# Latent keys through DRAM, and another order of the gate and up products

## The chip, the cores and the metric

The kernel runs on one core of a Trainium2 chip. The core has a matrix engine (TensorE, "PE" in the profile, with its weight loads shown apart as "PEld"), a vector engine (VectorE, DVE), a scalar engine (ScalarE, ACT), a general engine (GpSimd, POOL), and SyncE (SP), which issues all of this kernel's DMA transfers. The engines run beside each other and wait for each other through semaphores; each works through its own instructions in order. The metric is the device time of one execution in microseconds (us).

## The reference

Two layers work on `x` (1024 positions x 1024 columns, float32). Each has a mixer with three head groups (sliding-window attention A, latent attention B, spatial gating C) and a feed-forward block. The change touches group B and the first half of the feed-forward block:

```python
def mla(c_q, c_kv, k_rope, q_norm_w, w_uq, kv_norm_w, w_ukv, cos, sin):
    q = (rms_norm(c_q, q_norm_w) @ w_uq).reshape(b_, s_, 6, 64 + 32)
    q_nope, q_rope = q[..., :64], apply_rope(q[..., 64:], cos, sin)
    kv = (rms_norm(c_kv, kv_norm_w) @ w_ukv).reshape(b_, s_, 6, 64 + 64)
    k_nope, v = kv[..., :64], kv[..., 64:]
    k_r = apply_rope(k_rope[:, :, None, :], cos, sin)[:, :, 0, :]   # one for all heads
    ...
    sc = (q_nope . k_nope + q_rope . k_r) * 96 ** -0.5   # causal, then softmax, then times v

h = rms_norm(x, norm2_w[l]) * (1.0 + sc2) + sh2
gate, up = jnp.split(h @ w_gate_up[l], 2, axis=-1)       # 1024 x (2 x 2816)
x = x + g2 * ((jax.nn.silu(gate) * up) @ w_down[l])
```

`c_q` has 384 columns, `c_kv` 256, `k_rope` 32.

## The kernel before

**Number format.** Each float32 operand of a matmul is split in two parts, h (a rounded copy, by ScalarE) and lo (the rest, by VectorE: the operation in L139), and a product is three matmuls, h*h, h*lo, lo*h (`mm3`, L134 to L136).

**Who sets the order.** The stages are written as generators ("sequences"); hand-written strings of letters (`PRU0`, `PRU1` for the up-projection stage of layer 0 and 1, `PRB0`, `PRB1` for the heads stage) say which one makes its next step, and `need` pulls forward the steps that one depends on. The program is built from these steps by a planner that knows the buffers, so that the order on an engine can differ somewhat from the written one. Buffers come from pools with a fixed number of slots: `G` (33 slots of 4 KB in each partition), `W` (12), `R` (4), `SM` and `AD` (4 each), and eight PSUM banks (`PA`; four and two pairs, `PB`, in the heads stage).

**Up-projection of group B** (letters c, q, l, e, x, y). `ckv_seq` makes `c_kv` and `k_rope` of a tile of 128 positions (288 columns) and the factor `rs_kv` of its norm, and turns `k_rope`. `load_cq` fetches `c_q` from DRAM. `low_rank_t` (L803) transposes a tile's `c_q` (three blocks) and `c_kv` (two) on TensorE and splits them: `lowq`, `lowk`. `up_q` (L816) multiplies by `w_uq` and writes the queries, scaled by `rs_q` and turned, into `QK[t]`, with positions on partitions. `up_kv` (L830) does so with `w_ukv`: half 0 gives the keys of all heads (96 columns each for heads 0 and 1, with the turned `k_rope` copied in by GpSimd, L843; 64 for the others), which go into `QK[t]` beside the queries; half 1 gives the values, which are split into `vB`. Letter x steps through (t, half) of `up_q`, letter y through (t, half) of `up_kv`. `load_up` loads and splits the weights.

**Heads stage** (letters H, S, T, M). There are twelve groups: heads 0 to 5 with the second half of the queries (Q = 1, all 1024 keys), then heads 0 to 5 with the first half (Q = 0, 512 keys). `head_prep` (L1140) makes a group's operands with features on partitions: for each half of the keys that it needs, four transposes out of `QK` into a PSUM bank (`qkTB`, L1159), a rounded copy (L1160) and a subtraction (L139); and the same for the queries. `b_soft` makes the scores (`sB`) and the exponentials, `b_av` their transposes (`pTB`) and the product with `vB`. Keys of Q = 1 lie in two fixed buffers `kT1[h % 2]`, those of Q = 0 in `kT0[h % 2]`; group g is prepared once the scores of group g - 2 are written. The same stage loads x, `ya` and the output weights `wo`.

**Gate and up.** The product is done in 11 pairs of column blocks by a scheme of seven block products in place of eight. `left` (L1406) yields the seven left operands in order, with GpSimd subtracting or adding in place between them; `gu_prep` (L1461) splits each into `gus`; `gu_pair` (L1482) takes the products 0 to 6 with the right operands b11, b21, t3, t2, t1, b22, t4, each for gate and up (12 matmuls each). Products 0, 3, 4, 5 add up in banks `yy`, 1 has banks `xx`, 2 and 6 share `vv`. After 0 the sums are copied to `p1`; after 1 they are added to it and finished (Silu, multiply, store); after 3 copied to `u2` (L1523); after 4 copied to `u4` (L1528), added to `vv` and finished; after 5 finished; after 6 added to `u2` and finished. `want_gu` prepares weights some products ahead (`AHEAD`), and in `pair_steps` the hook `ahead` also runs two background jobs: `bg` (layer 0 only: loads `ada_w` and multiplies it up on VectorE, L256) and `bg2` (`wd_early`, splits down-projection weights into DRAM). The weights of the next pair are loaded in the fourth step of a pair into the four `R` slots (`gur`): `r0` holds a11 and a21, `r1` a12 and a22. Pair 0 runs within the heads strings (letter s).

Of the kernel before, what the change touches and what calls it, by code (L numbers as in the profile page):

```python
# [15 lines left out]
P = 128  # L16
# [50 lines left out]
EY = (1, 0, 1, 1, 0, 0, 0, 1)  # L67
AHEAD = (4, 2, 6, 10, 7, 9, 9)
# [10 lines left out]
def tile_trunk(ctx, tc, x, c, positions, ada_w, ada_b, norm1_w, w_in, a_sinks, b_q_norm_w, b_w_uq,  # L79
# [296 lines left out]
    cqd = [[dr.tile([P, 384], F32, name=f"cq{l}_{t}") for t in range(NT)] for l in range(DEPTH)]  # L376
    yad = [[dr.tile([P, 3, 512], F32, name=f"ya{l}_{hf}") for hf in range(2)] for l in range(DEPTH)]
# [175 lines left out]
    def layer(l, x_tiles):  # L553
# [228 lines left out]
        def load_up(k):  # L782
# [3 lines left out]
            DMA.dma_start(out=raw, in_=src[l, kk * P:(kk + 1) * P, :])  # L786
# [12 lines left out]
        def load_cq(t):  # L799
            cqs[t] = SM([P, 384], F32, "cqr")  # L800
            DMA.dma_start(out=cqs[t], in_=cqd[l][t])

        def low_rank_t(t):  # L803
            cq = cqs.pop(t)
            ck = ckv_tile(t)[:, 0:256]
            hq = G([P, 2, 3, P], F32R, "lowq")
            hk = AD("lowk", [P, 2, 2, P], F32R)
            for src, n, d in ((cq, 3, hq), (ck, 2, hk)):
                pv = PA("lowT").rearrange("p (b f) -> p b f", f=P)
                for k in range(n):  # L810
                    PE.transpose(pv[:, k, :], chunk(src, k), ident)
                ACT.copy(out=d[:, 0], in_=pv[:, :n, :])
                sub(DVE, d[:, 1], pv[:, :n, :], f32(d[:, 0]))
            low[t] = hq, hk

        def up_q(t, hf):  # L816
            d = low[t][0]
            if hf == 0:
                QK.append(G([P, 1024], F32, "QK"))
# [3 lines left out]
            for k in range(3):  # L823
                mm3(ps[:, :288], d[:, 0, k], d[:, 1, k], wuq[k][0][:, cs], wuq[k][1][:, cs], k == 0, k == 2)
# [5 lines left out]
        def up_kv(t, hf):  # L830
            d = low[t][1]
            g = QK[t]
            kd = g[:, 576:768].rearrange("p (h e) -> p h e", h=2)
            r = rs_kv[:, t:t + 1]
            ps = PA("ukv")
            for k in range(2):
                wv = [w.rearrange("p (h e) -> p h e", h=6)[:, :, hf * 64:hf * 64 + 64] for w in wukv[k]]
                mm3(ps[:, :384], d[:, 0, k], d[:, 1, k], wv[0], wv[1], k == 0, k == 1)
            if hf == 0:
# [232 lines left out]
        def cq_seq():  # L1072
            for t in range(NT):
                load_cq(t)
                yield
# [707 lines left out]
```

## Time and profile before

| | us |
|---|---|
| median of 3 runs | 2370.89 (2370.7 to 2372.88) |
| the profiled execution | 2370.5 |
| its span, first to last instruction | 2368.8 |
| TensorE busy | 2258.4 |
| VectorE busy | 1775.4 |
| ScalarE busy | 1120.9 |
| GpSimd busy | 984.8 |
| mean granted TensorE clock | 0.983 of full |

"Busy" of TensorE counts the latency of a matmul, so neighbouring matmuls overlap; the price of one more matmul is the distance from start to start. A row of waits reads: engine, tile and line that waited, what released it, microseconds in all, times, the longest. A row of windows reads: the stretch, then busy microseconds (and instructions) of PE, PEld, DVE, ACT, POOL, the granted clock, the DMA share and GB/s. A row in order of time reads: start, duration, engine, line, operation, how many in a row, and in brackets the idle time before it and its releaser. A row of a tile gives the shortest, median and longest duration in ns, first and last start, and the shapes.

### The profile page before, as it was taken

How to read it: one execution, taken by the hardware profiler on the slowest of the kernel's cores; microseconds unless marked ns; L12 is line 12 of the kernel's file. 1: busy time of each engine (PE TensorE's matmuls, PEld its weight loads, DVE VectorE, ACT ScalarE, POOL GpSimd, SP SyncE). 2: the span in 40 equal slices, each digit the busy share in tenths (PEclk: the TensorE clock that was granted, in tenths of full speed). 3: DMA queues.
4: the chain of work that ended last, by engine and by line, in shares of the span. 5: the costliest groups of instructions: out<-in, count | busy, mean ns of one | idle time of the engine just before them, and what ended most of it. 6: DMA issues, size and time to landing. Idle time of an engine off the chain costs nothing. (4 is left out here: it accounts for less than half of the span.)

```text
span 2368.8 us, 31988 instructions
## 1 busy us (share of the span) xinstructions
PE 2258.4 (95%) x11191; PEld 1904.2 (80%) x11191; DVE 1775.4 (75%) x2793; ACT 1120.9 (47%) x2296; POOL 984.8 (42%) x997
## 2 busy tenths in 40 slices
PE   5999899999999999999999899999999999999998
PEld 4789798887888777878878788988878888887786
DVE  7787578848767777699974875687588767638978
ACT  4566377636344344323344654784564444432233
POOL 4766630322323324545554655212224334225643
PEclk9999999999999999999999999999999999999999
DMA  6503432212566565862240253222134544468433
GB/s 255 167 19 110 175 132 90 90 54 89 173 213 232 186 232 187 319 253 89 80 158 19 62 172 143 81 81 98 54 110 177 180 169 169 171 223 287 150 109 114
DMA packets 155397, 347.66 MB, mean 147 GB/s; under 512 B 12522, under 2 KB 71652, under 8 KB 155236
## 3 DMA queue, kind: packets, MB, share of 16 engines
q1 hardware_dynamic: 155236, 345.62, 42.2%
q8 instruction: 88, 1.44, 0.3%
q14 instruction: 73, 0.60, 0.1%
HBM read 250.65 MB, written 94.92 MB: 146 GB/s over the span
## 5 line engine op out<-in xcount | busy, mean ns | idle before, releaser
L139 DVE TENSOR_TENSOR gus<-gur,gus 128x512 fp32r<-128x512 f32 x264 | 248.3, 961 | 60.3 <-ACT gus L142 59.5
L142 ACT CAST gus<-gur 128x512 fp32r<-128x512 f32 x264 | 160.7, 624 | 209.7 <-PE gate L136 77.0
L134 PE MATMUL gate<-hTh,gus 128*128 128x512 f32 x616 | 243.9, 396 | 15.2 <-ACT hTh L142 8.1
L134 PE MATMUL down<-dnt,dns 128*128 128x512 f32 x616 | 241.8, 393 | 11.5 <-issue 6.0
L134 PE MATMUL up<-hTh,gus 128*128 128x512 f32 x616 | 241.1, 391 | 3.8 <-ACT u L1528 3.8
L135 PE MATMUL down<-dnt,dns 128*128 128x512 f32 x616 | 241.1, 391 | 1.3 <-DVE dnt L139 1.3
L135 PE MATMUL gate<-hTl,gus 128*128 128x512 f32 x616 | 241.7, 392 | 0.1
L136 PE MATMUL gate<-hTh,gus 128*128 128x512 f32 x616 | 241.2, 392 | 0.0
L136 PE MATMUL down<-dnt,dns 128*128 128x512 f32 x616 | 240.7, 391 | 0.0
L136 PE MATMUL up<-hTh,gus 128*128 128x512 f32 x616 | 240.4, 390 | 0.0
L135 PE MATMUL up<-hTl,gus 128*128 128x512 f32 x616 | 240.2, 390 | 0.0
L1435 POOL TENSOR_TENSOR gur<-gur 128x512 f32<-128x512 f32 x44 | 65.2, 1482 | 398.8 <-DVE gus L139 369.5
L142 ACT CAST dns<-act 128x512 fp32r<-128x512 f32 x132 | 81.8, 622 | 248.6 <-PE down L136 189.6
L1613 DVE TENSOR_TENSOR x<-x,down 128x512 f32<-128x512 f32 x224 | 148.0, 679 | 28.9 <-PE down L136 28.6
L134 PEld LDWEIGHTS gate<-hTh,gus 128*128 128x128 f32 x616 | 116.9, 190 | 43.4 <-ACT u L1523 10.0
L139 DVE TENSOR_TENSOR dns<-act,dns 128x512 fp32r<-128x512 f32 x132 | 136.3, 1047 | 15.5 <-ACT dns L142 15.3
L134 PEld LDWEIGHTS down<-dnt,dns 128*128 128x128 f32 x616 | 116.2, 189 | 38.5 <-issue 6.8
L134 PEld LDWEIGHTS up<-hTh,gus 128*128 128x128 f32 x616 | 116.1, 189 | 28.7 <-ACT u L1528 4.9
L135 PEld LDWEIGHTS down<-dnt,dns 128*128 128x128 f32 x616 | 116.5, 189 | 25.8 <-DVE dnt L139 1.7
L135 PEld LDWEIGHTS gate<-hTl,gus 128*128 128x128 f32 x616 | 116.8, 190 | 25.2 <-DVE hTl L139 1.5
L136 PEld LDWEIGHTS gate<-hTh,gus 128*128 128x128 f32 x616 | 116.7, 189 | 24.5
L136 PEld LDWEIGHTS down<-dnt,dns 128*128 128x128 f32 x616 | 116.5, 189 | 24.5
(415 smaller groups left out, 6132.8 us busy)
## 6 DMA issues: line engine op xcount, KB each, us to landing
gur<-in_w_gate_up_dram SPq DMA_DIRECT2D x88, 512.0 KB
ada<-in_ada_w_dram SPq DMA_DIRECT2D x80, 512.0 KB
wp<-wpe SPq DMA_DIRECT2D x77, 512.0 KB
dnt<-wp SPq DMA_DIRECT2D x77, 512.0 KB
dnr<-in_w_down_dram SPq DMA_DIRECT2D x44, 512.0 KB
act<-act SPq DMA_DIRECT2D x44, 512.0 KB
wr<-in_w_in_dram SPq DMA_DIRECT2D x24, 512.0 KB
act<-u SPq DMA_DIRECT2D x44, 256.0 KB
```

What stands on the lines that cost most here:

```text
L134: PE.matmul(ps, lh, rh, start=start, stop=False, skip_group_check=more)
L135: PE.matmul(ps, lh, rl, start=False, stop=False, skip_group_check=more)
L136: PE.matmul(ps, ll, rh, start=False, stop=stop, skip_group_check=more)
L139: eng.tensor_tensor(out=out_, in0=a, in1=b, op=ALU.subtract)
L142: ACT.copy(out=h, in_=src)
L1435: return lambda o, a, b, op: eng.tensor_tensor(out=o, in0=a, in1=b, op=op)
L1613: DVE.tensor_tensor(out=av_, in0=av_, in1=ps[t], op=ALU.add)
```

## The change

**Keys.** `load_cq` scales `c_kv` in place by `rs_kv`. `low_rank_t` transposes also `k_rope` and stores its split to DRAM (`krd`); the split `c_kv` goes into buffers of four tiles (`kls`). `up_kv` is replaced by `up_v` (values of one tile) and `up_k` (128 features, that is two heads, of four tiles: weights stationary, 512 positions moving, so features come out on partitions), which splits the result and stores it to DRAM (`kd`). `head_prep` loads keys from `kd` and, for heads 0 and 1, `krd`; it transposes the queries only. The letter y steps through four values and three key chunks, twice: 14 steps where there were 16. `w_ukv` is loaded with keys and values apart.

**Gate and up.** Products run in the order 0, 2, 3, 1, 4, 6, 5 (pair 0: 0, 1, 2, 3, 4, 6, 5). After 2 the sum is copied to `v2`, to which 4 is added; `u4` is gone. The last product of a pair (5) is issued after the first of the next. `bg` runs in the first four steps of a pair.

```diff
+ORD = ((0, 1, 2, 3, 4, 6, 5), (0, 2, 3, 1, 4, 6, 5))
...
+    kd = [dr.tile([2, 384, S], F32, name=f"kd{l}") for l in range(DEPTH)]
+    krd = [dr.tile([2, 32, S], F32, name=f"krd{l}") for l in range(DEPTH)]
...
+                for a in range(2):
+                    DMA.dma_start(out=raw[:, 384 * a:384 * a + 384].rearrange("p (h e) -> p h e", h=6),
+                                  in_=src[l, kk * P:(kk + 1) * P, :].rearrange("p (h a e) -> p h a e", h=6, a=2)[:, :, a, :])
...
         def load_cq(t):
             cqs[t] = SM([P, 384], F32, "cqr")
             DMA.dma_start(out=cqs[t], in_=cqd[l][t])
+            ck = ckv_tile(t)[:, 0:256]
+            DVE.tensor_scalar(out=ck, in0=ck, scalar1=rs_kv[:, t:t + 1], scalar2=None, op0=ALU.mult)
...
         def low_rank_t(t):
...
+            pv = PA("lowT").rearrange("p (b f) -> p b f", f=P)
+            for k in range(2):
+                PE.transpose(pv[:, k, :], chunk(ck, k), ident)
+            PE.transpose(pv[:32, 2, :], ck[:, 256:288], ident)
+            ACT.copy(out=kh[:, :, ts_], in_=pv[:, :2, :])
+            sub(DVE, kl[:, :, ts_], pv[:, :2, :], f32(kh[:, :, ts_]))
+            ACT.copy(out=hq[:32, 6], in_=pv[:32, 2, :])
+            sub(DVE, hq[:32, 7], pv[:32, 2, :], f32(hq[:32, 6]))
+            DMA.dma_start(out=krd[l][:, :, t * P:(t + 1) * P].rearrange("a p f -> p a f"), in_=f32(hq[:32, 6:8]))
...
+        def up_v(t):
+            kh, kl = kls[t // 4]
+            ts_ = slice(t % 4 * P, (t % 4 + 1) * P)
+            ps = PA("uv")
+            for k in range(2):
+                mm3(ps[:, :384], kh[:, k, ts_], kl[:, k, ts_], wukv[k][0][:, 384:], wukv[k][1][:, 384:], k == 0, k == 1)
+            v = G([P, 6, 2, 64], F32R, "vB")
...
+        def up_k(hf, c):
+
+            kh, kl = kls[hf]
+            ps, cs = PA("uk"), slice(c * P, (c + 1) * P)
+            for k in range(2):
+                mm3(ps, wukv[k][0][:, cs], wukv[k][1][:, cs], kh[:, k, :], kl[:, k, :], k == 0, k == 1)
+            kk = G([P, 2, 512], F32R, "kk")
+            ACT.copy(out=kk[:, 0], in_=ps)
+            sub(DVE, kk[:, 1], ps, f32(kk[:, 0]))
+            DMA.dma_start(out=kd[l][:, cs, hf * 512:(hf + 1) * 512].rearrange("a p f -> p a f"), in_=f32(kk))
...
+        def up_kv_seq():
+            need("e", 5)
+            for hf in range(2):
+                for t in range(4 * hf, 4 * hf + 4):
+                    need("l", t + 1)
+                    up_v(t)
+                    yield
+                for c in range(3):
+                    up_k(hf, c)
                     yield
...
+            for i, dst in enumerate((kh, kl)):
+                if h < 2:
+                    DMA.dma_start(out=f32(dst[64:96]), in_=krd[l][i, :, :512 * (Q + 1)])
+                DMA.dma_start(out=f32(dst[:64]), in_=kd[l][i, 64 * h:64 * h + 64, :512 * (Q + 1)])
+            for _ in range(Q + 1):
+                yield
+            pq = PA("qkTB")
+            for i in range(4):
+                PE.transpose(pq[:96, i * P:(i + 1) * P], QK[Q * 4 + i][:, h * 96:(h + 1) * 96], ident)
+            ACT.copy(out=q2[:96, 0], in_=pq[:96])
+            sub(DVE, q2[:96, 1], pq[:96], f32(q2[:96, 0]))
+            yield
...
+                elif i == 2:
+                    for m in range(2):
+                        v2[m] = SM([P, 512], F32, "v2")
+                        ACT.copy(out=v2[m], in_=vv[m])
+                elif i == 3:
+                    for m in range(2):
+                        u2[m] = SM([P, 512], F32, "u2")
+                        ACT.copy(out=u2[m], in_=yy[m])
+                elif i == 4:
+                    for m in range(2):
+                        DVE.tensor_tensor(out=v2[m], in0=v2[m], in1=yy[m], op=ALU.add)
+                    finish(v2[0], v2[1], 1, 1)
...
-                    if 7 * (j - 1) + i < 9 or i in (1, 3, 4, 6):
+                    if 7 * (j - 1) + i < 9 or i < 4:
...
+        def first_products(g, n):
+
+            for _ in range(2 * n):
+                run(g)
+                yield
+            open_pair.append(g)
...
         for j in range(1, NJ):
-            drain(pair_steps(j))
+            g = pair_steps(j)
+            run(g, 2)
+            drain(open_pair.pop())
+            drain(first_products(g, 5))
+        drain(open_pair.pop())
```

More of the change, by code (lines that the diff above doesn't have):

```diff
@@ new lines, in up_v @@
+        def up_v(t):
+            kh, kl = kls[t // 4]
+            ts_ = slice(t % 4 * P, (t % 4 + 1) * P)
+            ps = PA("uv")
+            for k in range(2):
+                mm3(ps[:, :384], kh[:, k, ts_], kl[:, k, ts_], wukv[k][0][:, 384:], wukv[k][1][:, 384:], k == 0, k == 1)
+            v = G([P, 6, 2, 64], F32R, "vB")
+            vB.append(v)
+            pv = ps[:, :384].rearrange("p (h e) -> p h e", h=6)
+            ACT.copy(out=v[:, :, 0, :], in_=pv)
+            sub(DVE, v[:, :, 1, :], pv, f32(v[:, :, 0, :]))
@@ L1150, in head_prep @@
             heads[h, Q] = (q2[:, 0], q2[:, 1], kh, kl)
-            q0 = h * 96
-            k0 = 576 + 96 * h if h < 2 else 768 + 64 * (h - 2)
-            kn = 96 if h < 2 else 64
-            todo = [(hf, k0, kn, kh[:, hf * 512:hf * 512 + 512], kl[:, hf * 512:hf * 512 + 512])
-                    for hf in range(Q + 1)] + [(Q, q0, 96, q2[:, 0], q2[:, 1])]
-            for hf, c0, n, dh, dl in todo:
-                pq = PA("qkTB")
-                for i in range(4):
-                    PE.transpose(pq[:n, i * P:(i + 1) * P], QK[hf * 4 + i][:, c0:c0 + n], ident)
-                ACT.copy(out=dh[:n], in_=pq[:n])
-                sub(DVE, dl[:n], pq[:n], f32(dh[:n]))
-                yield
+            for i, dst in enumerate((kh, kl)):
[3 more added lines that the diff above has]
+            for _ in range(Q + 1):
+                yield
+            pq = PA("qkTB")
[4 more added lines that the diff above has]
+            yield
         def b_soft(h, n, sm, pr):
@@ L1459, in load_gu, with gu_prep @@
             return r
-        def gu_prep(raws):
+        def gu_prep(raws, order):
             gens = []
@@ L1504, in finish @@
                 DMA.dma_start(out=actd[l][2 * j + m][:, b, :], in_=g)
-            yy = banks()
-            yield from products(0, "b11", yy, True)
-            for m in range(2):
-                ACT.copy(out=p1[:, m, :], in_=yy[m])
-            yield
-            xx = banks()
-            yield from products(1, "b21", xx, True)
-            for m in range(2):
-                DVE.tensor_tensor(out=p1[:, m, :], in0=p1[:, m, :], in1=xx[m], op=ALU.add)
-            finish(p1[:, 0, :], p1[:, 1, :], 0, 0)
@@ L1516, in gu_pair @@
-            yield
-            vv = banks()
-            yield from products(2, "t3", vv, True)
-            yield
-            yield from products(3, "t2", yy, False)
-            for m in range(2):
-                u2[m] = SM([P, 512], F32, "u2")
-                ACT.copy(out=u2[m], in_=yy[m])
-            yield
-            yield from products(4, "t1", yy, False)
-            for m in range(2):
-                u4[m] = SM([P, 512], F32, "u4")
-                ACT.copy(out=u4[m], in_=yy[m])
-            for m in range(2):
-                DVE.tensor_tensor(out=u4[m], in0=u4[m], in1=vv[m], op=ALU.add)
```

143 lines of the change are left out of this document (69 added, 74 removed).

## The prediction

> **What bounds the kernel now.** I read the page first (busy shares), then 10 and 60 us windows to find stages with gaps, then TensorE's waits by stage, then single tiles and the order of time for the price of one instruction.
>
> ```profile
> span 2368.8 us, 31988 instructions
> PE 2258.4 (95%) x11191; PEld 1904.2 (80%) x11191; DVE 1775.4 (75%) x2793; ACT 1120.9 (47%) x2296; POOL 984.8 (42%) x997
> 360.00:420.00 60.00, 59.76 (x395) 51.34 (x394) 51.41 (x111) 47.82 (x101) 4.91 (x5) 1.00 0.26 89
> ```
>
> TensorE works in 95% of the span; 110 us are gaps. In the heads stage of layer 0 (third row, columns span, PE, PEld, DVE, ACT, POOL, clock, DMA) it has no gaps, so there an instruction taken off TensorE is time won, and VectorE is next at 51.4 of 60. Elsewhere the gaps count. TensorE's waits, four rows from the up-projection stages (180 to 326 us; layer 1, 1320 to 1510), then gate and up of layer 0 (560 to 990) and of layer 1:
>
> ```profile
> PE uq L136 <- DVE lowq L139: 4.8, 1, 4.8
> PE uq L134 <- ACT lowq L812: 2.2, 1, 2.2
> PE uq L135 <- DVE upl L147: 2.3, 1, 2.3
> PE ukv L134 <- ACT uph L146: 1.9, 1, 1.9
> ...
> PE gate L134 <- ACT u L1523: 6.3, 5, 1.8
> PE up L134 <- ACT u L1528: 3.8, 2, 2.1
> PE gate L134 <- ACT u L1523: 0.6, 1, 0.6
> ```
>
> The last three are the copies of the running sums out of PSUM after products 3 and 4 (L1523, L1528): the next product adds to the same bank and must wait. They are 10.1 us in layer 0 and 0.6 in layer 1.
>
> **Keys: what goes.** One head group transposes keys in runs of four. The tile view counts one cast per run:
>
> ```profile
> L1160 ACT CAST kTh<-qkTB x24: 562/582/604, 326.5 to 1551.7; 64x512 fp32r<-64x512 f32 x16, 96x512 fp32r<-96x512 f32 x8
> L1160 ACT CAST kT<-qkTB x12: 565/572/582, 388.7 to 1606.9; 64x512 fp32r<-64x512 f32 x8, 96x512 fp32r<-96x512 f32 x4
> L139 DVE TENSOR_TENSOR kTl<-qkTB,kTh x24: 670/673/687, 327.1 to 1552.8; 64x512 fp32r<-64x512 f32 x16, 96x512 fp32r<-96x512 f32 x8
> ...
> 331.33 0.60 PE L1159 MATMUL qkTB<-ident,QK 128*64 128x128 f32 x4
> 331.69 0.46 PE L134 MATMUL sB<-kTh,qT 96*128 96x448 f32 x1
> 331.99 0.37 PE L135 MATMUL sB<-kTl,qT 96*128 96x448 f32 x1
> 332.19 0.37 PE L136 MATMUL sB<-kTh,qT 96*128 96x448 f32 x1
> ```
>
> 24 + 12 = 36 runs of keys, 144 transposes. The busy time of a run (0.60) holds the latency of its last; the price is from start to start: 331.69 - 331.33 = 0.36 us for four, and the first matmul behind them takes 0.30 (331.99 - 331.69) where the next takes 0.20, 0.10 more. 36 x 0.46 = 16.6 us; if runs stand side by side and only the transposes count, 36 x 0.36 = 13.0. I take **-16.0**. With them go 36 casts of 0.58 and 36 subtractions of 0.67 us, 21 and 24 us of ScalarE and VectorE beside TensorE: nothing in the sum.
>
> **Keys: what comes.** 16 transposes of the rotary 32 columns, beside the two of `ck`, at 0.36 / 4: **+1.4**. The key half of the up-projection was 96 matmuls of 384 columns and becomes 72 of 512:
>
> ```profile
> 263.06 0.34 PE L135 MATMUL ukv<-upl,lowk 128*128 128x384 f32 x1
> 263.23 0.34 PE L136 MATMUL ukv<-uph,lowk 128*128 128x384 f32 x1
> ...
> 266.05 0.40 PE L134 MATMUL uv<-wh,TH 128*128 128x512 f32 x1
> 266.28 0.39 PE L135 MATMUL uv<-wl,TH 128*128 128x512 f32 x1
> ```
>
> 72 x 0.23 - 96 x 0.17 = 16.6 - 16.3: **+0.3**. The scaling of `ck` (16 more VectorE instructions of 128x256), the 12 casts and subtractions of 128x512 in place of 32 scaled copies, and 16 rotary casts and subtractions stand in the up-projection:
>
> ```profile
> 240.00:300.00 60.00, 53.03 (x292) 47.42 (x291) 36.58 (x66) 24.68 (x59) 38.69 (x54) 0.91 0.48 167
> ```
>
> VectorE and ScalarE have 23 and 35 us of 60 free there, so I cost them at nothing; TensorE's matmuls hide them. They are in order behind other work, though: if that cover fails, it is a wait like the 4.8 above that grows, and it is held in the term on the up-projection below. GpSimd loses its 16 copies of the rotary part into `QK`, which no row above waits for.
>
> **The road through DRAM.** A key chunk is cast (0.58), subtracted (0.67), stored, loaded. The nearest row for a transfer on a waiting path:
>
> ```profile
> 1420.65 0.33 SPq L786 DMA_DIRECT2D upr<-in_b_w_ukv_dram  x1
> ...
> 1423.81 0.94 ACT L146 ACTIVATE uph<-upr,cols 128x768 fp32r<-128x768 f32 x1 [0.48 <-DMA upr<-in_b_w_ukv_dram]
> ```
> ```profile
> 317.88 0.29 PE L136 MATMUL uq<-uph,lowq 128*128 128x288 f32 x1
> 318.01 0.29 PE L134 MATMUL uq<-uph,lowq 128*128 128x288 f32 x1
> ```
>
> 3.2 us from issue to use, for 384 KB. Twice that with cast and subtraction is 7.6 us from the last matmul of `up_k(1, 0)` to the first score of head 0. By the written order, two key units (six matmuls of 0.23) and at least five query units (nine of 0.13) come between: 2 x 1.4 + 5 x 1.2 = 8.8 us in either layer. So it is just hidden, unless a transfer ahead in the queue delays it or the load waits for the last chunk's store too. Bounds per layer: 0 and 7.6 us; I take 1.5, nearer to hidden: **+3**.
>
> Later heads load keys one group ahead. SP issues every transfer in order, and two key loads now wait there for the scores of the head before last; behind them queue the loads of x, `wo` and `ya`, which nobody needs for long. The reverse matters:
>
> ```profile
> SPq L1260 <- PE qkTB L1159: 47.2, 2, 23.7
> ```
>
> SP already sits 23.7 us, once a layer, on a load of x whose buffer the transposes of `QK` free. A key load behind such a wait comes when TensorE has passed that point, so the wait alone doesn't starve it, but it can come with less lead. The six groups of layer 0 with all keys stand between the casts at 326.5 and 388.7, 10 us each against 3.2; the six later ones are shorter, with half the keys to load. In bytes it is little: 10 MB of loads and 6 of stores in a kernel whose DMA share in the heads stage is 0.26. Bounds over 24 groups 0 and 24 x 3.2; I take the row's hidden case with one miss: **+1**.
>
> The weights `w_ukv` are now loaded in runs of 64 numbers, 256 bytes, and no row shows such a load alone; it is between nothing and another landing of 3.2 us on the path of layer 1, where TensorE waits 1.9 for these weights. I take nothing and keep the end. The Trainium skill ("DMA: Bandwidth & Descriptors", section "Why small descriptors are slow (HBM only)") puts a 256-byte piece at 27% overhead; by it the estimate would be a fraction of a microsecond for each load, and nothing in the sum changes sign.
>
> **Up-projection, rearranged.** Tile order of keys and values is no longer (t, half) but four values, three key chunks, twice, so `low_rank_t(3)` is needed four steps in where it was seven. The G buffers carry `kls`, `kk` more; cq loads can queue behind the new small stores. The waits there (4.8, 2.2, 2.3, 1.9: 11.2 us) are drawn anew: bounds -11 and, as the stage has as many places to wait as before, +11. I take **0**.
>
> **Gate and up.** Why ScalarE's copy was late, and what a wait costs beyond its length:
>
> ```profile
> 774.59 0.63 ACT L1502 ACTIVATE u<-u 128x512 f32<-128x512 f32 x1 [5.14 <-DVE u L1530]
> 775.12 0.57 ACT L1528 COPY u<-up 128x512 f32<-128x512 f32 x1
> ```
> ```profile
> 775.74 0.50 PE L134 MATMUL up<-hTh,gus 128*128 128x512 f32 x1 [2.06 <-ACT u L1528]
> 777.48 0.63 PE L134 MATMUL up<-hTh,gus 128*128 128x512 f32 x1
> 777.90 0.63 PE L135 MATMUL up<-hTl,gus 128*128 128x512 f32 x1
> ```
> ```profile
> 770.00:780.00 10.00, 7.94 (x29) 6.07 (x28) 8.69 (x7) 2.12 (x4) 7.55 (x5) 0.85 0.23 79
> 1940.00:1950.00 10.00, 10.00 (x46) 8.29 (x45) 8.25 (x13) 4.45 (x8) 0.00 (x0) 1.00 0.39 151
> ```
>
> ScalarE sat 5.14 us on a Silu that waited for VectorE, with the second copy behind it; TensorE lost 2.06 us and then ran at 0.42 us a matmul instead of 0.23 for a while: 29 in ten microseconds against 46, 17 x 10/46 = 3.7 us lost for a wait of 2.06. So the seven waits are 10.7 us by length, and with this one's slow clock 12.3. The number of copies, adds, Silus and stores of a pair is unchanged (`v2` takes the place of `u4`); only their places move. The new order puts one product (24 matmuls, 5.4 us per half, 10.9) between 3 and 4, one between 4 and 6, two between 4 and 5; waits of 2 us after a delay of 5 us vanish. What is late next is either VectorE's reads after 4 and 6, or weights: their steps 0, 2 now stand together, and step 2 waits for GpSimd, which waits for VectorE. Rows of that kind:
>
> ```profile
> POOL gur L1435 <- DVE gus L139: 380.6, 37, 31.2
> ACT gus L142 <- DMA gur<-in_w_gate_up_dram: 40.3, 22, 5.1
> ```
>
> TensorE waited for no `gus` in the rows above, and step 2 no longer needs the second loaded tile (`r1`), so the 5.1 us waits shrink. The last product of a pair, held until after the first of the next, keeps its two weight tiles and two banks for 11 us more, and the ada and down-weight work is now called in a pair's first four steps; neither lies on a wait above. I count 1.3 given back: **-11** (bounds -12.3 and 0). Of the clock the Trainium skill ("TensorE: Matmul & The Clock Gate", section "HAM oscillation — how this bites in real kernels") says that gaps over about 3.4 us throttle it; here one of 2.06 did, so the measurement decides. By the page the waits would be worth 10.7, not 12.3.
>
> **Sum.** -16.0 + 1.4 + 0.3 + 3 + 1 + 0 - 11 = -21.3. The profiled execution took 2370.5 us (span 2368.8 and 1.7 around it): 2349.2. It stands 0.4 below the median shown, 2370.89. **Forecast 2349**, own range 2342 to 2357.
>
> **Rivals.**
> - *The hand-over only moves* (0.14). The first product of a pair is followed by the last of the pair before, and then by a product into new banks: a bank must be free within one half product, as now, and Silu and multiply are in order behind other work. For it: VectorE is at 8.7 of 10 in the bad window. Against: layer 1 with the same exposure lost 0.6 only, and the new distances are longer. Gate and up win nothing: 2349 + 11 = 2360.
> - *The up-projection gets worse* (0.13): waits there double (+11.2) or weights land late. 2349 + 11 = 2360, with a slow clock up to 2367.
> - *Those waits vanish* (0.12): 2349 - 11 = 2338.
> - *Keys come late at every group* (0.11). One mechanism: the loads queue on SP behind loads that wait for a buffer, so a part of the 3.2 us isn't covered at each of the 24 groups. It decides from (21 + 5) / 24 = 1.1 us a group; at half a landing, 1.6 us, it is 2349 - 1 + 38 = 2386, slower. For it: the 23.7 us wait. Against: one group of lead.
>
> **How the numbers follow.** Forecast 0.50, the rest as given. A measurement here can tell about 0.2% from no change, 4.7 us. The 2360 cases reach above 2366 in a quarter of their 0.27: same 0.07. Slower 0.11, faster 0.82. The range 2336 to 2367 leaves out the late keys and half of the best case's and a little of the worse case's tail.
>
> **What would show it.** Right: no key transposes, 16 more in `lowT`, heads stages 7 to 8 us shorter each, no TensorE wait on u copies in layer 0's gate and up, with 46 matmuls in each 10 us. Wrong: TensorE waiting for a DMA of keys (kTh, kT), above all at the start of the heads or at every group of the second half of queries; TensorE waiting for `gus`, or for Silu or VectorE at a pair's second product; longer waits on lowq.

## The result, and the profile after

The changed kernel takes 2384.49 us (median of 5 runs, 2382.23 to 2391.25) against 2372.88 (5 runs, 2370.70 to 2375.98) of the kernel before: a ratio of 1.0053, 95% interval 1.0037 to 1.0069. It is slower by half a per cent, where 21 us less were forecast. The profiled execution took 2382.23 us. The page of the changed kernel, its head:

```profile
span 2380.5 us, 31760 instructions
PE 2247.9 (94%) x11039; PEld 1888.3 (79%) x11039; DVE 1774.4 (75%) x2801; ACT 1096.8 (46%) x2256; POOL 976.9 (41%) x981
```

TensorE has 152 matmuls and 10.5 busy us less than before, and the span is 11.7 us longer: its gaps grew from 110 to 133 us. The two halves of the heads stage of layer 0, queries 512 to 1023 and then 0 to 511, in windows of before and of after (stretch, length, busy us and instructions of PE, PEld, DVE, ACT, POOL, clock, DMA share, GB/s):

```profile
328.60:397.90 69.30, 69.17 (x440) 60.22 (x441) 60.98 (x115) 54.58 (x105) 5.04 (x4) 1.00 0.24 80
397.90:457.00 59.10, 58.88 (x380) 50.98 (x379) 51.51 (x123) 46.15 (x109) 16.96 (x12) 1.00 0.28 92
```
```profile
331.50:397.10 65.60, 64.00 (x388) 54.36 (x389) 52.99 (x102) 48.52 (x92) 5.02 (x4) 1.00 0.29 79
397.10:461.50 64.40, 59.67 (x373) 50.42 (x372) 51.78 (x122) 47.05 (x107) 15.59 (x12) 1.00 0.49 164
```

The first half is 3.7 us shorter, the second 5.3 longer: TensorE now has gaps of 1.6 and 4.7 us where it had 0.1 and 0.2. A part of this is the cut between the halves: five value products, six transposes of probabilities and two matmuls of `sq`, which stand ahead of it in before, stand behind it in after. So it is their sum that tells. TensorE's waits of after in the up-projection of layer 0 and of layer 1, then in gate and up of layer 0:

```profile
PE uq L135 <- ACT lowq L827: 6.8, 1, 6.8
...
PE lowT L826 <- DMA cqr<-cq: 4.8, 1, 4.8
...
PE qkTB L1192 <- POOL QK L363: 2.9, 2, 2.3
PE avA L958 <- DVE pLA L140: 2.8, 2, 1.8
...
PE gate L135 <- ACT u L1562: 9.9, 2, 5.3
```

In layer 1 three waits are new or longer: for the load of cq, for the rotary work on the last query tile, and for the attention's subtractions (pLA). The copies of u, now L1562, still hold TensorE in layer 0. The rotary wait stands at the entry of layer 1's heads. The first 12 us behind the first score there, in after and, for comparison, in `after_values_last`, an experiment told below in which that wait is gone:

```profile
1518.00:1524.00 6.00, 6.00 (x20) 5.25 (x21) 3.27 (x7) 3.67 (x6) 0.00 (x0) 0.57 0.00 0
1524.00:1530.00 6.00, 6.00 (x36) 5.46 (x35) 4.06 (x10) 3.76 (x8) 0.00 (x0) 0.86 0.40 90
```
```profile
1518.00:1524.00 6.00, 5.68 (x32) 4.81 (x32) 4.56 (x9) 4.36 (x7) 1.02 (x2) 1.00 0.00 0
1524.00:1530.00 6.00, 6.00 (x42) 5.58 (x41) 5.25 (x13) 5.08 (x12) 0.00 (x0) 1.00 0.40 90
```

Behind the gap the granted clock of after was 0.57 and 0.86, and TensorE had 56 matmuls in place of 74.

The table cuts the span at the first or last TensorE instruction of a tile (us), beside three experiments that are told below.

| from, to | before | after | keys_only | gate_up_only | before_ck_scaled |
|---|---|---|---|---|---|
| start, first ckv (layer 0) | 177.1 | 176.0 | 178.3 | 178.5 | 177.3 |
| first ckv, first score | 151.5 | 155.5 | 156.1 | 151.4 | 153.0 |
| first score, first gate | 202.8 | 204.2 | 204.8 | 202.8 | 202.8 |
| first gate, first down | 455.4 | 459.1 | 455.4 | 455.7 | 455.9 |
| first down, first ckv (layer 1) | 360.3 | 357.4 | 361.1 | 359.8 | 360.4 |
| first ckv, first score | 155.6 | 165.8 | 165.8 | 157.3 | 161.7 |
| first score, first gate | 202.7 | 205.7 | 205.0 | 202.7 | 202.7 |
| first gate, last up | 436.7 | 435.8 | 436.6 | 435.0 | 436.7 |
| last up, last down | 217.8 | 212.1 | 216.4 | 212.1 | 216.4 |

The first row is the same code in all of them: one execution scatters by 2.5 us there. Later rows scatter too where the code is the same: from the first gate to the first down, the eleven kernels with the new gate and up order and ada's steps where after has them take 455.3 to 460.6 us, so the 3.7 us that after is longer there are no finding. The change lost 14.2 us in the up-projection stages and 4.4 in the heads, and won most in the last down projection.

### The profile page after: what moved, and what is told of

Read it like the earlier page. It is cut to its first block, busy times and chain, and to the rows that moved or that the text cites. A ratio compares the mean times of both kernels' runs of the same rounds, so it can differ in the third digit from the quotient of the medians.

```text
span 2380.5 us, 31760 instructions
## 1 busy us (share of the span) xinstructions
PE 2247.9 (94%) x11039; PEld 1888.3 (79%) x11039; DVE 1774.4 (75%) x2801; ACT 1096.8 (46%) x2256; POOL 976.9 (41%) x981
## 5 line engine op out<-in xcount | busy, mean ns | idle before, releaser
L140 DVE TENSOR_TENSOR gus<-gur,gus 128x512 fp32r<-128x512 f32 x264 | 234.2, 902 | 119.2 <-ACT gus L143 114.8
L143 ACT CAST gus<-gur 128x512 fp32r<-128x512 f32 x264 | 160.3, 624 | 205.6 <-DVE acc L257 56.4
L135 PEld LDWEIGHTS down<-dnt,dns 128*128 128x128 f32 x616 | 115.7, 188 | 35.4 <-ACT dnt L143 7.0
L1467 POOL TENSOR_TENSOR gur<-gur,s 128x512 f32<-128x512 f32 x44 | 68.0, 1552 | 181.8 <-DVE gus L140 181.8
L135 PEld LDWEIGHTS up<-hTh,gus 128*128 128x128 f32 x616 | 116.0, 188 | 27.5 <-ACT u L1562 3.7
L137 PEld LDWEIGHTS up<-hTh,gus 128*128 128x128 f32 x616 | 115.7, 188 | 24.1
```

What stands on the lines that cost most here:

```text
L135: PE.matmul(ps, lh, rh, start=start, stop=False, skip_group_check=more)
L137: PE.matmul(ps, ll, rh, start=False, stop=stop, skip_group_check=more)
L140: eng.tensor_tensor(out=out_, in0=a, in1=b, op=ALU.subtract)
L143: ACT.copy(out=h, in_=src)
L1467: return lambda o, a, b, op: eng.tensor_tensor(out=o, in0=a, in1=b, op=op)
```

## The experiments

Times are medians, with the ratio to the kernel before on the same chip and its 95% interval. A stage's length comes from the profile of the run.

### The two parts alone

`keys_only` and `gate_up_only` are the kernel before with the keys' part of the diff, and with the rest of it.

> The keys part of the change alone, gate and up as before. The two traces, stage by stage, put these differences (after less before) on the keys: layer 0 up-projection +3.4, heads +0.9, layer 1 ckv and up-projection +9.7 from the start of ckv to the end of uq, heads +3.4; sum +17.4. Theory A (the loss is the keys', gate and up win about 5 with their new entry to the down projection): 17 us slower than before, about 2390. Rival B (loss and gain mix, since buffers and queues carry over from stage to stage): the keys alone are within 6 us of before. The prediction on record had the keys at 10 us faster.

> The gate and up part alone (order 0,2,3,1,4,6,5, last product late, ada work in a pair's first four steps), keys as before. Theory A: layer 0 gate and up +3.7 us as in the trace of after, layer 1 -0.7, the first products of down -2.8 and -5.9: 5 to 6 us faster than before, about 2367, and two to three waits of TensorE of 3 to 5 us each on ScalarE's copies of u (L1562 in after). Rival B (the waits in layer 0 come from the keys' shift of 5 us against the background work): gate and up of layer 0 lose nothing here, 10 us faster, about 2363. The prediction on record had 11 us faster.

Measured: keys_only 2391.26 us, 1.0098 (1.0082 to 1.0113); gate_up_only 2364.87 us, 0.9976 (0.9966 to 0.9985). In the whole time theory A holds for both: the keys lose 21 us, gate and up win 5.5 (the two sum to more than the whole change lost; the intervals overlap). The 3.7 us that theory A took layer 0's pairs to lose are not there. gate_up_only is faster than both kernels, and no later one beat it. Its gain isn't where the prediction had it: the pairs of layer 0 win nothing, those of layer 1 1.7, the last down projection 5.7 (4.3 against the other two kernels with the old order). The second and third ten microseconds of that projection in before, with TensorE's gap of 2.5, and in after:

```profile
2152.00:2162.00 10.00, 7.48 (x34) 5.92 (x33) 10.00 (x9) 2.38 (x4) 8.04 (x4) 1.00 1.01 393
2162.00:2172.00 10.00, 10.00 (x39) 8.06 (x38) 7.85 (x12) 1.82 (x4) 3.20 (x1) 0.83 0.55 202
```
```profile
2169.40:2179.40 10.00, 10.00 (x46) 8.29 (x45) 10.00 (x12) 2.39 (x4) 5.15 (x3) 1.00 0.98 372
2179.40:2189.40 10.00, 10.00 (x45) 8.28 (x45) 10.00 (x11) 2.39 (x4) 3.74 (x2) 1.00 0.83 320
```

91 matmuls in place of 73: the gap and the slow clock behind it (0.83) are gone. Which part of the new order does this (the other last product, or its late place) was not tried.

### Heads: are the transposes worth their time on TensorE?

`no_key_transposes`, before without those of heads 2 to 5:

```diff
             for hf, c0, n, dh, dl in todo:
+                if h >= 2 and n == 64:
+                    yield
+                    continue
```

> The kernel before, with the key transposes, casts and subtractions left out for heads 2 to 5 (those heads use the keys of heads 0 and 1; the output is another). 12 runs of four in each layer are gone, and nothing comes in their place: no DRAM, no loads. Theory A (the transposes were work that filled TensorE's waits for the softmax chain, so taking them away shortens nothing): each heads stage is within 2 us of before, about 2371. Rival B (TensorE sets the stage; in the changed kernel it was the loads that took the gain away): 24 x 0.46 = 11 us faster, about 2361.

`after_dummy_transposes`, the reverse:

```diff
-            for _ in range(Q + 1):
+            for hf in range(Q + 1):
+                pq = PA("qkTB")
+                for i in range(4):
+                    PE.transpose(pq[:64, i * P:(i + 1) * P], QK[hf * 4 + i][:, h * 96:h * 96 + 64], ident)
                 yield
```

> The changed kernel with TensorE's key transposes put back where they stood, four of 128x64 for each run, into a bank that nobody reads: no casts, no subtractions; keys still come from DRAM. 18 runs of four in each layer, 0.46 us each by the prediction, 8.3 us of TensorE a layer. Theory A (the time that the transposes took on TensorE is free in the changed kernel, as its heads stage waits for the softmax chain): from the first score to the last value product 130 to 132 us as in after, within 3 us of after in all, about 2384. Rival B (TensorE sets the stage there too, and something else slowed it): 136 to 138 us in each layer, 13 to 16 us slower than after, about 2399.

Loads left out (`after_no_key_loads`: the load from `kd` moves under `if h < 2`), loads issued by GpSimd (`after_keys_on_gpsimd_queue`: `POOL.dma_start` for both), and no key preparation at all in the second half, in either kernel (`kh, kl = [v[:, :512] for v in kT1[h % 2]]` for Q == 0):

> The changed kernel with the loads of keys for heads 2 to 5 left out (they use the keys of heads 0 and 1; the output is another); keys are still projected and stored. From the first score to the last value product the heads stage took 128.4 us in both layers of before, 130.0 and 131.6 in after, and 124.3 and 124.2 in no_key_transposes. Theory A (the loads, or the places that they take on SP's queue, cost what the missing transposes had won): 124 us in both layers, 11 to 13 us faster than after, about 2372. Rival B (the loads are hidden; TensorE's gaps are the softmax chain's, in the order that the planner now chose): 129 to 132 us, within 4 us of after, about 2384.

> The changed kernel with the loads of keys in the heads stage (L1186, L1187) issued by GpSimd in place of SP, so that nothing queues behind them on SP. In after the second half of the heads stage (queries 0 to 511) takes 64.4 and 65.6 us in the two layers, 59.1 and 60.1 in before; SP waits 55 us on these loads, and the loads of x, ya and wo come behind them. Theory A (those late loads make the gaps of the second half): 60 us or less in both layers, 8 to 10 us faster than after, about 2375. Rival B (the gaps are the softmax chain's, with the key transposes no longer between its parts): 63 to 66 us, within 3 us of after. Rival C (a load from GpSimd's queue takes longer): TensorE waits for a DMA of keys, slower than after.

> The kernel before with no key preparation for the second half of the heads stage (queries 0 to 511): those heads use the first 512 columns of the keys that the first half left (the output is another). No DRAM is involved; 6 runs of transposes, casts and subtractions a layer are gone. The second half takes 59.1 us in before, 57.8 in no_key_transposes (4 of the 6 runs gone), 63.4 to 65.2 in the kernels whose keys come from DRAM. Theory A (without the transposes between them, the softmax chain's parts follow each other in another order and wait for each other): 62 to 65 us, the loss with no DRAM at all. Rival B (the loads into kT0, whose buffer comes free late, make the loss): 57 us or less.

> The changed kernel with the same: no loads of keys for the second half, which uses the first 512 columns of the keys of the first half (the output is another). Theory A: 62 to 65 us in the second half, as in after (64.4 and 64.8). Rival B: 57 us or less, and the first half as in after, 65 to 67.

Measured, layer 0 / layer 1, in us (the halves meet at VectorE's 25th maximum over scores; the rest ends at the first gate product):

| kernel | time, ratio | first half | second half | rest | sum |
|---|---|---|---|---|---|
| before | | 69.3 / 69.3 | 59.1 / 59.1 | 74.4 / 74.3 | 202.8 / 202.7 |
| no_key_transposes | 2373.65, 1.0014 (1.0004 to 1.0023) | 66.5 / 66.4 | 57.8 / 57.8 | 76.8 / 76.8 | 201.1 / 201.0 |
| before_half_without_keys | 2373.83, one run | 69.6 / 69.6 | 59.1 / 59.0 | 76.7 / 76.8 | 205.4 / 205.4 |
| after | 2384.49, 1.0053 | 65.6 / 66.8 | 64.4 / 64.8 | 74.2 / 74.1 | 204.2 / 205.7 |
| after_no_key_loads | 2386.76, 1.0050 (1.0031 to 1.0068) | 68.1 / 67.6 | 63.8 / 63.7 | 74.3 / 74.3 | 206.2 / 205.6 |
| after_keys_on_gpsimd_queue | 2387.53, 1.0066 (1.0051 to 1.0081) | 69.4 / 67.5 | 63.7 / 63.8 | 74.3 / 74.3 | 207.4 / 205.6 |
| after_half_without_keys | 2388.99, one run | 67.9 / 66.8 | 61.9 / 61.9 | 78.3 / 76.7 | 208.1 / 205.4 |
| after_dummy_transposes | 2392.23, 1.0094 (1.0080 to 1.0108) | 68.8 / 68.9 | 65.2 / 64.1 | 74.1 / 74.1 | 208.1 / 207.1 |

Read the sums against the TensorE work taken out, at the prediction's 0.46 us a run:

- `no_key_transposes` drops 5.5 us a layer and wins 4.1 up to the last value product. Then 2.4 are given back before the gate: TensorE waits once for the residual addition of x, in the row below this list, and four more matmuls of the out-projection are left over. In layer 0 the pairs took another 3.7 in this one execution (459.1 us from the first gate to the first down). As a whole it isn't faster, as theory A has it; but up to the last value product the work wasn't free.
- `before_half_without_keys` drops 2.8 us and takes 2.6 more. Its two halves are as long as those of before, with 3.0 us of gaps on TensorE where before has 0.3, and the rest has the same wait for x. Its 59.1 us lie between theory A (62 to 65) and rival B (57 or less). `after_half_without_keys`, at 61.9, is nearly theory A's.
- The dummies put back 8.3 us a layer and cost 3.9 and 1.4 in the heads by one profile each, most of it in the first half. By the ratios the whole kernel is 0.4% or 10 us slower than after (1.0094 against 1.0053, each known to 0.15%), for 16.6 us of work. This lies between theory A (within 3 us) and rival B (13 to 16).
- Taking the loads away, or off SP's queue, wins nothing: rival B in both.

```profile
PE oAB L134 <- DVE x L1280: 1.2, 1, 1.2
```

So TensorE's time is a part of what sets the stage, and not all of it. Three of TensorE's gaps in the second half of before_half_without_keys, in order of time:

```profile
416.47 0.39 PE L134 MATMUL sB<-kTh,qT 96*128 96x256 f32 x1 [0.90 <-DVE nmB L1176]
...
421.58 0.44 PE L1220 MATMUL avB<-pTs,vB 128*128 128x384 f32 x1 [1.00 <-DVE pTs L139]
...
436.59 0.50 PE L1219 MATMUL avB<-pTs,vB 128*128 128x512 f32 x1 [0.68 <-ACT pTs L1198]
```

and the same place in after:

```profile
418.51 0.39 PE L135 MATMUL sB<-kT,qT 96*128 96x256 f32 x1 [0.67 <-DVE nmB L1209]
419.36 0.33 PE L1228 MATMUL pTB<-ident,pB 128*128 128x128 f32 x1 [0.23 <-ACT pB L1212]
423.62 0.44 PE L1253 MATMUL avB<-pTs,vB 128*128 128x384 f32 x1 [1.00 <-DVE pTs L140]
429.46 0.50 PE L136 MATMUL oAB<-wo,yTh 128*128 128x512 f32 x1 [0.98 <-DMA wo<-wo]
```

All but the last row are links of the softmax chain: a score bank waits for VectorE's maximum, a transpose of probabilities for ScalarE's exp, a value product for the split of what was transposed. The last row waits for a load of the output weights. The same links are waited for in the kernel that has no DRAM road. In before TensorE has none of these waits between the first score and the last value product; in after they come to 4.0 and 3.8 us in the two layers, and with the dummies to 2.9 and 2.4. That fits with transposes that had filled them; no run changed the order of the chain itself.

### Up-projection: the scaling of ck, and where it stands

`before_ck_scaled` is before with this alone. Behind it the results are copied without a scale, and a `need`, as in after, has a tile's ckv made ahead of it; TensorE's operations in that stage of layer 1 keep their order but for a few neighbours:

```diff
             DMA.dma_start(out=cqs[t], in_=cqd[l][t])
+            ck = ckv_tile(t)[:, 0:256]
+            DVE.tensor_scalar(out=ck, in0=ck, scalar1=rs_kv[:, t:t + 1], scalar2=None, op0=ALU.mult)
```

> The kernel before with one part of the change: ck scaled in place on VectorE when cq is loaded (16 instructions of 0.35 us, which wait for GpSimd's rstd), and the three results of the key and value projection copied without a scale. Keys are transposed as in before. Theory A (these instructions stand in VectorE's order ahead of the attention's subtractions and the casts, and what waits behind them moves TensorE): in layer 1 from the first ckv to the first uq 71 us in place of 67.1 (76.1 in after), and 3 to 6 us slower than before. Rival B (VectorE has room): 67 us there, within 2 us of before; the late start is the load of cq behind that of w_ukv.

Measured: 2378.52 us, 1.0027 (1.0015 to 1.0040), and 75.1 us from the first ckv to the first uq of layer 1 (67.1 in before, 76.1 in after; theory A asked for 71). Theory A holds. VectorE in order of time, from this run:

```profile
1390.10 0.71 DVE L803 TENSOR_SCALAR ckv<-ckv,rskv 128x256 f32<-128x256 f32 x1 [1.62 <-POOL rskv L172]
1390.73 0.54 DVE L139 TENSOR_TENSOR pLA<-pTA,pHA 128x384 fp32r<-128x384 f32 x1
...
1409.81 1.38 DVE L803 TENSOR_SCALAR ckv<-ckv,rskv 128x256 f32<-128x256 f32 x1 [1.64 <-POOL rskv L172]
1411.11 1.85 DVE L147 SCALAR_TENSOR_TENSOR upl<-upr,cols,uph 128x576 fp32r<-128x576 f32 x1
```

The instruction itself is short; it sits 1.6 us on GpSimd's rstd with pLA and upl behind it, and TensorE needs both. Its waits in that stretch, in before and in this run:

```profile
PE lowT L811 <- DMA cqr<-cq: 0.8, 1, 0.8
...
PE avA L934 <- DVE pLA L139: 0.5, 2, 0.3
```
```profile
PE lowT L813 <- DMA cqr<-cq: 3.5, 1, 3.5
...
PE avA L933 <- DVE pLA L139: 2.7, 2, 1.7
```

The load of cq stands on SP behind that of `w_ukv`, which now waits 4.8 us for VectorE in place of 1.6; so cq is issued 64.0 us behind the first ckv in place of 57.7.

Three more runs changed one thing in after: the scaling on GpSimd (`POOL.tensor_scalar`), the rotary store behind the second query product, and `w_ukv` in one load, sorted by two casts and two subtractions.

> The changed kernel with the scaling of ck (16 instructions, L811 in after) on GpSimd in place of VectorE. In layer 1 two of them stand on VectorE ahead of the attention's subtractions and wait there 1.0 and 1.6 us for GpSimd's rstd, and TensorE waits 2.8 us for those subtractions; the stretch from the first ckv to the first product of the gate branch is 52.4 us, 48.8 before. Theory A (that place in VectorE's order is the 3.6 us): 49 us there, and 3 to 4 us faster than after, about 2380. Rival B (the stretch is set by the loads of weights, whose buffers come free later): 52 us, within 2 us of after.

> The changed kernel with the store of the rotary part (L837 in after) issued behind the second query product of its tile, so that SP no longer waits for its subtraction. SP waits 26.7 us in layer 0 and 17.7 in layer 1 on these stores in after, with loads of cq behind them. Theory A (the cq loads come late because they queue behind those stores): TensorE's wait for a DMA of cqr in layer 1 (4.8 us) goes and the two up-projection stages, 109.4 and 113.4 us from the first product of the gate branch to the first score, lose 6 us together; about 2378. Rival B (the first cq load queues behind a load of w_ukv that waits for a buffer, and the rest is the new order of TensorE's work): the 4.8 us stay, within 2 us of after.

> The changed kernel with w_ukv loaded as before, one contiguous load for each half of the rows, and sorted into keys and values by the casts and subtractions (two of 128x384 each in place of one of 128x768). Theory A (the loads in pieces of 256 bytes land late): the waits of TensorE on uph and upl in layer 1 (3.8 us) shrink and cq, which queues behind, comes earlier; 2 to 4 us faster than after, about 2381. Rival B (the loads in small pieces cost nothing on the path, as forecast): within 2 us of after.

Measured, in this order: 2389.20, 1.0058 (1.0043 to 1.0074); 2388.86, 1.0055 (1.0037 to 1.0072); 2387.72, 1.0045 (1.0028 to 1.0062). None can be told from after. On GpSimd the wait for pLA falls to 0.7 us, but the stretch to the first product of the gate branch takes 56.3 in place of 52.4, and both theories (49 and 52) miss: TensorE waits 2.5 us for the attention's casts instead, and ScalarE 7.0 us for GpSimd in place of 2.5. The cq wait stays at 4.6 with late stores, so SP's small stores aren't its cause. With whole loads it is 3.5: the small pieces may cost it about a microsecond, which the medians can't show.

Two runs changed the order: `after_values_last` takes both halves' key chunks ahead of the last four values, and `after_scale_late_values_last` does that in layer 1 alone and ties the scaling to the arrival of cq.

```diff
+            rk = TN(1, "rk")
+            DVE.scalar_tensor_tensor(out=rk, in0=cq[:, 0:1], scalar=0.0, in1=rs_kv[:, t:t + 1], op0=ALU.mult, op1=ALU.add)
+            DVE.tensor_scalar(out=ck[:, 0:256], in0=ck[:, 0:256], scalar1=rk, scalar2=None, op0=ALU.mult)
```

> The changed kernel with the up-projection of keys and values in another order: four values, all six key chunks, then the last four values, each behind the queries of its tile, so that the last rotary work and the road of the keys through DRAM have value products beside them. In after TensorE waits at the first heads for the rotary work on the last QK tile (0.8 us in layer 0, 2.9 in layer 1). Theory A (the order at the end of the up-projection costs this much and more behind it, as the first transposes of probabilities come 1.9 us later still in layer 1): 4 to 6 us faster than after, about 2380. Rival B (the stage's loss lies ahead of its end, in the late start of the low-rank transposes): those waits go, but it is within 2 us of after.

> The changed kernel with two repairs: the scaling of ck is held until the cq tile has landed, directly ahead of the transposes that use it (a one-column VectorE instruction makes it depend on cq), so that it no longer stands ahead of the attention's subtractions; and in layer 1 alone the last four values come after all key chunks. Theory A (the scaling's place costs 6 to 8 us in layer 1 and 1 to 2 in layer 0, the end of layer 1's up-projection 5): from the first ckv to the first uq of layer 1 68 to 70 us (76.1 in after, 67.1 in before), 9 to 13 us faster than after, about 2373. Rival B (what is late then is the next thing, as everything in the stage is): within 4 us of after.

Measured: 2382.20, 1.0038 (1.0023 to 1.0053); 2400.63, 1.0128 (1.0113 to 1.0142). With values last, layer 1 takes 292.4 us from the first ckv to the last value product (297.4 in after, 284.0 in before), layer 0 289.1 (285.5 in after, 279.9 in before): the end of the stage is worth 5 us in layer 1, as theory A has it, and layer 0 gives most of it back, so that the whole can't be told from after. Of the 5 us only 1.0 lie ahead of the first score. The other 3.9 lie in the heads, which take 201.8 us to the first gate in place of 205.7: there the rotary wait at their entry and the slow clock behind it are gone (the rows above). The other kernel with values last in layer 1 has 202.2 there. The late scaling (76.1 us from the first ckv to the first uq, where theory A had 68 to 70) misses both theories; TensorE's waits of that run in layer 0 and in layer 1:

```profile
PE lowT L832 <- DVE ckv L829: 19.9, 4, 11.9
```
```profile
PE lowT L832 <- DVE ckv L829: 15.4, 4, 6.2
```

Early, the scaling delays what stands behind it on VectorE; late, it is itself behind VectorE's other work and TensorE waits for it.

### Gate and up: why the copies of u are still late

ScalarE of after, then VectorE, at the longest wait (5.3 us, at 937):

```profile
935.37 1.14 ACT L143 CAST gus<-gur 128x512 fp32r<-128x512 f32 x2 [9.14 <-DVE acc L257]
936.42 0.58 ACT L1562 COPY u<-gate 128x512 f32<-128x512 f32 x1
```
```profile
934.01 1.28 DVE L257 SCALAR_TENSOR_TENSOR acc<-ada,cact,acc 128x1024 f32<-128x1024 f32 x1 [6.50 <-DMA ada<-in_ada_w_dram]
```

A cast ahead of the copy waits for a buffer that the multiply of ada frees, and the multiply for its load. Four variants of gate_up_only: ada's steps spread again (`i in (1, 3, 4, 6)` for `i < 4`), most of them moved behind the pairs (`if 7 * (j - 1) + i < 13`), multiplied on GpSimd (a `tensor_scalar` and an addition), or the first eight moved ahead into the out-projection (a letter for `bg` eight times in `PRB0`).

> As gate_up_only, but the background work of ada goes back to steps 1, 3, 4 and 6 of a pair, in place of the first four. Theory A (the waits on u in layer 0 come from ada's multiplies, bunched with the load of the next pair's weights: ScalarE's cast waits for a buffer that VectorE's multiply frees, and that multiply for its load): the waits of 3 to 5 us go, ScalarE's idle time before casts of gus put to VectorE's acc falls from 56 us to under 30, and it is 6 to 10 us faster than gate_up_only, about 2358. Rival B (the new product order itself leaves the copy late): the same waits, within 3 us of gate_up_only.

> As gate_up_only, but of the background work of ada only the first 13 steps run within the pairs of layer 0; the rest runs alone between gate and up and the down projection. The time as a whole will be worse; what counts is the stretch from the first gate product of layer 0 to the last up product, 455.2 us in before and in gate_up_only. Theory A (ScalarE's copies of u come late since the casts ahead of them wait for buffers that ada's multiplies free): the stretch loses the 10 us of waits and their slow clock and takes 445 to 447. Rival B (the waits come from the order of products itself, or move to the next thing that is late): 452 or more.

> As gate_up_only, with ada's multiplies of layer 0's pairs on GpSimd, a multiply by the column and an addition for each, in place of one VectorE instruction. GpSimd is busy 156 of 455 us there, VectorE 352. Theory A (VectorE's multiplies make ScalarE's copies of u late, and GpSimd has room): the stretch from the first gate product of layer 0 to the last up product, 455.2 us in gate_up_only and 436.6 in gate_up_no_ada, comes to 445 to 450, 5 to 10 us faster than gate_up_only, about 2357. Rival B (GpSimd is in order behind its subtractions that wait for VectorE, so the buffers of ada come free still later): 455 or more, slower than gate_up_only.

> As gate_up_only, with the first eight steps of layer 0's background work of ada (a load of 512 KB and one multiply of 1.28 us on VectorE each) moved ahead, into the end of the out-projection, where VectorE is busy 41 of 74 us. gate_up_no_ada lost 27 of the 40 steps from the pairs and its stretch was 18.6 us shorter, 0.7 us a step. Theory A (a step costs the pairs what it keeps ScalarE's casts waiting, and VectorE has room in the out-projection): the pairs' stretch 455.2 falls by 4 to 6 us and the out-projection stays at 74 us; 4 to 6 us faster than gate_up_only, about 2360. Rival B (the steps delay the residual additions and the norm of the second half's start, or hold buffers of the W pool): what is won is given back, within 2 us of gate_up_only or slower.

Measured, in this order: 2367.48, 0.9985 (0.9977 to 0.9994); 2389.12, 1.0065 (1.0050 to 1.0080); 2459.91, 1.0376 (1.0362 to 1.0391); 2368.44, 0.9988 (0.9979 to 0.9997). TensorE's waits in gate and up of layer 0, of gate_up_only, gate_up_spread and gate_up_no_ada:

```profile
PE gate L135 <- ACT u L1530: 8.6, 2, 5.2
...
PE up L135 <- ACT u L1530: 1.2, 1, 1.2
```
```profile
PE up L135 <- ACT u L1530: 8.0, 4, 2.5
...
PE gate L135 <- ACT u L1530: 3.0, 2, 1.8
```
```profile
PE gate L135 <- ACT hTh L143: 4.1, 1, 4.1
PE hT L485 <- DVE p L1521: 1.1, 1, 1.1
```

Without ada's steps no wait for u is left, and the pairs take 436.6 us in place of 455.4, of which the gaps are 10. TensorE's own share of ada, which moves too, and the granted clock (0.99 over the stretch in place of 0.98) make up the rest: ada is the cause. Spread, the waits are shorter and more (11.0 against 9.8 us): its bunching, my first theory, is not. The steps must stand somewhere: behind the pairs they cost 38 us, on GpSimd the pairs take 94 more, ahead of them the stretch from the last value product to the last up product takes 536.1 in place of 529.8. No other place that was tried for them is better.

## Why the prediction was wrong, step by step

- **Key transposes, -16.0.** This step failed: "there an instruction taken off TensorE is time won", read from a stage in which TensorE has no gaps. Each heads stage was to be 7 to 8 us shorter; they are 1.4 and 3.0 longer. Taken out alone, two thirds of the transposes, 11.0 us by the price used, won 8.2 up to the last value products, 3.4 up to the gates, and nothing in the whole kernel. Dummies in their place cost 5.3 of 16.6 us in the heads and about 10 in the whole. A stage where TensorE is always busy and VectorE is 86% busy can be held by both and by the chain between them.
- **The road through DRAM, +3 and +1.** The mechanism was right: TensorE waits for a load of keys once, 0.8 us. The loads of `wo`, "which nobody needs for long", are waited for 1.0 and 0.9 us. The rival that keys come late at every group is out, by the loads left out and by the other queue.
- **Scaling, casts and stores, nothing.** This failed too. The prediction named the cover ("TensorE's matmuls hide them") and that they are in order behind other work; it counted free VectorE time, not what stands behind an instruction that waits. Alone it costs 7.6 us by stages (1.5 and 6.1), 6.2 by medians.
- **Up-projection, 0 within 11.** 14.2 us, outside the bounds, as they held only the four waits that were there. The scaling is about half. Of the other 6.6, the order at the end of layer 1's stage is worth 1.0 (and 3.9 more in the heads behind it); the rest, 2.5 in layer 0 and 3.1 in layer 1, has no single cause that a run shows.
- **Gate and up, -11.** -5.5, by another way. This step failed too: in layer 0 the waits for the copies of u, which were to vanish, are 9.8 us in gate_up_only. The rival *the hand-over only moves* came true there in its outcome, nothing won, but by another mechanism: the copies of u wait for the casts, the casts for ada, of which the prediction said that it lies on no wait. That the 5.14 us wait on a Silu was only the last of several late things fits with this, but no run shows it for the old order. The gain came in the down projection, which the prediction didn't price; that half of the forecast number came is luck. A small slip: 10.7 us are the seven waits of layer 0 (10.1) and one of layer 1.
- **What stays open.** Why the heads of after aren't shorter than those of before, by anything near 8.3 us a layer. Layer 1's 3.0 us longer are for the most part the entry: with values last, and so without the gap and the slow clock there, it takes 0.9 less than before. Layer 0, whose clock is full there, is 1.4 longer, and 0.3 with values last. Without key work in the second half both kernels take 205.4 in layer 1, but the two sums are made of other parts, so this shows only that a loss can come without the road. The order of the chain is what is left of what I thought of; no run set that order by hand.

## What to carry to other kernels

A full TensorE row doesn't say that all work taken off it is won: before counting such work, take that work out alone, or put dummies in its place, and see whether the stage's length answers, and what the stage behind it gives back. Look also at the gap at a stage's entry and at the granted clock behind it before looking for the loss inside. An instruction on an engine with room costs what waits behind it while it waits, so look at its own operands' time and at its successors, not at the engine's busy share. Where a wait names one late step, ask what is late next before counting its length as a gain.

## What the hardware showed that was not expected

GpSimd took 2.98 us for a multiply of 128x1024 by a column and 2.48 for the addition, where VectorE does both in 1.45. The rows of gate_up_ada_on_gpsimd, and VectorE's subtraction in gate_up_only and in this run (count, busy us and mean ns):

```profile
L257 POOL TENSOR_SCALAR ada<-ada,cact 128x1024 f32<-128x1024 f32 x35 | 104.2, 2978 | 61.2 <-DMA ada<-in_ada_w_dram 61.1
L258 POOL TENSOR_TENSOR acc<-acc,ada 128x1024 f32<-128x1024 f32 x35 | 86.9, 2482 | 2.4
```
```profile
L140 DVE TENSOR_TENSOR gus<-gur,gus 128x512 fp32r<-128x512 f32 x130 | 112.3, 878 | 43.4 <-ACT gus L143 39.4 <-DMA act<-v 2.2
L257 DVE SCALAR_TENSOR_TENSOR acc<-ada,cact,acc 128x1024 f32<-128x1024 f32 x35 | 50.6, 1445 | 24.8 <-DMA ada<-in_ada_w_dram 24.8
```
```profile
L140 DVE TENSOR_TENSOR gus<-gur,gus 128x512 fp32r<-128x512 f32 x130 | 130.1, 1011 | 186.9 <-ACT gus L143 183.2 <-DMA act<-v 2.2
```

The same 130 subtractions went from 0.88 to 1.01 us with GpSimd busier. The Trainium skill ("SBUF — State Buffer", section "🎯 Summary: rules for kernel authors") says that when VectorE has two SBUF inputs while a GpSimd operation reads SBUF, the second to issue is blocked until the first ends. The trace agrees in direction: the mean grows by 0.13 us. But the 11 products behind the first Silu of a pair, VectorE with two SBUF inputs in the same stretch, went from 1.03 to 0.88 us, so the cause isn't shown. It is the smaller part of that run's 95 us; ScalarE's casts behind GpSimd's additions are the larger.
